# Row tiles for two small products, keys copied between halves by transfers, and an order table for the planner, in a two-layer attention trunk

## The chip, the core and the metric

The kernel runs on one core of a Trainium2 chip. The metric is the device time of one execution in microseconds; the time given for a kernel is the median of its runs. A core has a matrix engine (TensorE; PE in the profile, with its weight loads as PEld), a vector engine (VectorE, DVE), an activation engine (ScalarE, ACT), GpSimd (POOL) and a sync engine that issues most transfers (SyncE, SP). Each works through its own instructions in the order in which they were written.

## What is computed

Two residual layers over a sequence of 256 tokens of width 1024. Each takes shift, scale and gate from a condition vector, normalises, mixes, projects and adds. Cut to the places that the change touches:

```python
for i in range(DEPTH):                       # two layers
    shift, scale, gate = jnp.split(cond @ ada_w[i] + ada_b[i], 3, axis=-1)
    h = rms_norm(x, norm_g[i]) * (1 + scale[:, None, :]) + shift[:, None, :]
    y = nsa_mixer(h, ...) if i == 0 else moba_mixer(h, ...)
    x = x + gate[:, None, :] * y
# first layer: 16 query heads in 4 groups, three branches, each with its own keys
p_cmp = masked_softmax(q @ k_cmp * scale)    # 15 compressed blocks per group
o = g0 * (p_cmp @ v_cmp) + g1 * o_slc + g2 * o_win
y = (o * silu(z)) @ w_out
# second layer: one branch of plain causal attention, same grouping
y = (softmax(causal(q @ k * scale)) @ v * silu(z)) @ w_out
```

All inputs and the output are float32.

## The kernel before, in words

**Precision.** Large products are made of float32r parts: an operand is split into hi and lo, and a product is hi·hi + hi·lo + lo·hi, three one-pass matmuls (`product`, lines 757 to 766; `parts_of`, 624 to 631: ScalarE casts hi, VectorE subtracts lo). Small products are plain float32, which PE runs as two passes, so one instruction of the program appears as two in the trace.

**Stages.** The condition's modulation for layer one and the first projection run interleaved while weights stream in (to about 60 us). Then come the remaining projections of the first layer, with the compression network beside them; the first layer's attention over eight head pairs (`pair_a`, 1290 to 1331) with the z projection as filler; its output projection (`out_products`, 1370); the second layer's norm and projections; its attention (`pair_b`, 1439) with its z projection as filler; and the last output projection. The second layer's modulation (`ada_rows`, 640) runs beside the first layer's attention, column-tiled: four products of 32 output rows stand side by side in four column strips of the array (`tile_position=(0, 32 * j)`).

**Compressed values.** `compressed(hf)` (1262) makes, for four pairs at a time, the softmax over the compressed blocks and leaves it transposed in `pcT[hf]`, 128 rows: 32 rows for each of the four pairs, 16 for each head. The values are in `Vbd` (1239): for each half and pair a 128 x 128 matrix that is zero but for that pair's 32 rows, built with `emask`, eight columns of ones over 16 rows each. In `pair_a` line 1328 multiplies the whole 128 rows of `pcT` by the pair's matrix and opens the pair's output bank `o`, into which `values` (899) then adds the other two branches, column-tiled in two strips of 64. `gated` reads `o` and frees it.

**Gate spread.** `ada_gate(0)` (696) has the gate in four rows of a tile `g`, two partial sums and a bias row in each half. Lines 714 to 718 spread it to all 128 partitions with two matmuls against `selG`, whose two 128 x 128 matrices hold ones over the upper or the lower 64 rows.

**Second layer's keys.** `make_k` (820) normalises and rotates the keys, doubles each 64-wide key to 128 columns (`twice`), transposes four groups for each 128 tokens, so that both halves of the partitions hold the key, and splits the result into hi and lo in `KTB`, a view of the tile KTA. Both halves are needed because a query column holds its hi part over its lo part. The first layer's keys go the same way.

**What sets the order.** Nothing is issued while the program is written down: `Plan.record` collects operations, and `Plan.issue` (231) then simulates the engines with costs (`_cost`, 174) and picks, engine by engine, the ready operation that can start first, ties broken by level (`FIRST_OF_ALL`, `URGENT`, `CHAIN`, `FILL`) and then by the number under which the operation was recorded. It also hands out the tile buffers of each tag: `ps` has six PSUM banks and `acc` two, `raw` has five buffers for weights on their way in. A load waits until its buffer is free. All engine instructions thus carry one line in the profile, L373, the line of the planner that calls them.

Of the kernel before, what the change touches and what calls it, by code (L numbers as in the profile page):

```python
# [9 lines left out]
F32 = mybir.dt.float32  # L10
# [4 lines left out]
OP = mybir.AluOpType  # L15
# [21 lines left out]
DEEP = 2e4  # L37
TILED, LATER = -0.5, 0
SHORT_ROWS, SMALL, BEHIND, EARLY_RATE = 1.1, 7e4, 5500.0, 348.0
ISSUE, FIRST_BYTE, RATE, LANDED = 450.0, 1500.0, 315.0, 700.0  # L40

# [11 lines left out]
class Plan:  # L53
# [120 lines left out]
    def _cost(self, engine, method, args, kw, aps):  # L174
# [15 lines left out]
        if engine == "T":  # L190
            if method == "transpose":
                return 262.0 if aps[1].dtype == F32 else 180.0
            cols = free(aps[2])
            if aps[2].dtype == F32:
                m = free(aps[1])
                if "tile_position" in kw and m <= 64:
                    return max(cols * 4.28 * max(32, m) / P, 60.0)
                return 2 * max(cols * 2.14, 264.0)
            return max(cols * (1.07 if aps[2].dtype == F32R else 1.0), 264.0)
# [31 lines left out]
    def issue(self, opening=()):  # L231
# [46 lines left out]
        for op in ops:  # L278
            op["at"] = 0.0
            if not op["wait"]:  # L280
                ready[op["engine"]].append(op)
        done = 0
        while done < len(ops):
            best = None
            for e, ops_e in ready.items():
# [4 lines left out]
                for op in ops_e:  # L290
                    t = max(clock[e], op["at"])
                    if first is not None and t > first and not (op["level"] < 0 and t <= first + self.AHEAD):
                        continue
                    blocked = False
                    for n in op["needs"]:
                        r = room(n)
                        if r is None:
                            blocked = True
                            break
                        t = max(t, r)  # L300
                    if blocked:
                        continue
                    found.append((t, self._rank(op, e, mode), op["id"], op))
                    first = t if first is None else min(first, t)
# [28 lines left out]
            if e == "T":  # L333
                tick = int(start // TICK)
                if op["mode"] != mode:
                    cost += 240.0
                mode = op["mode"]
                cost = cost * (1 / 2.4 if tally.get(tick - 1, 0.0) >= 3060.0 else 1 / 1.2)
                tally[tick] = tally.get(tick, 0.0) + op["cost"]
            end = start + cost  # L340
            clock[e] = end
            seen = end + self.SEEN[e]
            if "bytes" in op:
                if e != "S":
                    seen = start + (BEHIND if op["level"] > 0 else 2400.0)
                else:
                    wire = max(wire, start + ISSUE + FIRST_BYTE) + op["bytes"] / (EARLY_RATE if start < 5e4 else RATE)
                    seen = wire + (450.0 if start < 5e4 else LANDED)
                    landings.append(seen)
                    if start < DEEP:  # L350
                        clock[e] = max(start + ISSUE, landings[-8] if len(landings) >= 8 else 0.0)
# [49 lines left out]
def kernel(  # L401
# [47 lines left out]
    plan.tag("early", early["pool"], 1024, 12)  # L449
    plan.tag("raw", work, 1024, 5)  # L450
    plan.tag("hi", work, 1024, 4, F32R)
# [76 lines left out]
    for m in range(2):  # L528
        keep(maskC[:, m, :], [[-16, 16]], m * P - 31)
    selG = const.tile([P, 2, P], F32, name="selG")  # L530
    nc.gpsimd.memset(selG, 0.0)
    nc.gpsimd.memset(selG[0:64, 0, :], 1.0)
    nc.gpsimd.memset(selG[64:128, 1, :], 1.0)
    ones = const.tile([P, P], F32, name="ones")
    nc.gpsimd.memset(ones, 1.0)
    identR = const.tile([P, P], F32R, name="identR")
    V.tensor_copy(identR, identF)
    emask = const.tile([P, 8], F32, name="emask")
    V.tensor_reduce(emask, identF.rearrange("p (j n) -> p j n", n=16), axis=AX.X, op=OP.add)

# [155 lines left out]
    def ada_gate(l):  # L696
# [12 lines left out]
        else:  # L709
            g = yield from ada_rows(l, (2 * D, 2 * D + 512), 512)  # L710
            for s in range(2):
                Q.dma_start(g[64 * s + 1:64 * s + 2], bias[:, s * 512:(s + 1) * 512])
            mix, src = (selG[:, 0], selG[:, 1]), (g, g)
        for s in range(2):
# [105 lines left out]
    def make_k(raw_k, kinds, kt_view, offs):  # L820
# [5 lines left out]
        norm_rope(src, 2 * n, KVH, TC[:, j0:j0 + n].rearrange("p c m d -> p (c m) d"),  # L826
                  TS[:, k0:k0 + n].rearrange("p c m d -> p (c m) d"), y)
        for j, off in enumerate(offs):
            twice = tile_of("y", KVH, 2 * HD)
# [408 lines left out]
    vb = tile_of("ps", 512)  # L1238
    Vbd = const.tile([P, 2, 4, P], F32, name="Vbd")
    for hf in range(2):  # L1240
        for cc in range(2):
# [4 lines left out]
                     start=(cc == 0), stop=(cc == 1))  # L1246
        V.tensor_mul(Vbd[:, hf].rearrange("p j (e d) -> p (j e) d", e=2),
                     vb[:, None, hf * HD:(hf + 1) * HD].to_broadcast([P, 8, HD]),
                     emask[:, :, None].to_broadcast([P, 8, HD]))

# [8 lines left out]

    pcT = {}  # L1260

# [28 lines left out]
    def pair_a(i):  # L1290
# [28 lines left out]
        for r in (1, 0):  # L1319
# [6 lines left out]
            pT.insert(0, p_transposed(block))  # L1326
        o = tile_of("ps", 512)
        T.matmul(o[:, 0:S], Vbd[:, hf, j_], pcT[hf], start=True, stop=False)
        vs = slice(g * HD, (g + 1) * HD)
# [171 lines left out]
```

## Time and profile before

| | us |
|---|---|
| median of 3 runs | 317.1 |
| lowest, highest run | 315.71, 317.89 |
| the profiled execution, its own time | 317.45 |
| its span, first to last instruction | 315.7 |

How to read it: a row of the timeline has its start, its length, the engine, the line, the operation, output tile <- input tiles, rows x columns of the stationary operand and of the output, and how many instructions it merges. Names are those of the tiles without their numbers: `ps` and `acc` are PSUM banks, `pT` transposed probabilities, `HT` the transposed layer input, `raw` weights as loaded, `hi` and `lo` their parts, `qg` queries, `condz` the condition. A shape `128*32` is a matmul in a column tile of 32, `128*64` one in a tile of 64. Ends of matmuls are modelled and overlap the next start. A row of busy times by stage has, for each engine, the busy time and the number of instructions.

### The profile page before, as it was taken

To read this page: it belongs to the slowest core of one execution; us is meant where nothing else is said; L and a number is where in the kernel's file an instruction comes from. 1 tells how busy PE (TensorE), PEld (TensorE's weight loads), DVE (VectorE), ACT (ScalarE), POOL (GpSimd) and SP (SyncE) were. 2 spreads that over 40 slices of the span, in tenths; PEclk is the share of its full clock that TensorE was granted. 3 is DMA by queue.
4 is the path that set the end of the run, shared out by engine and by line. 5 is a ranking of instruction groups with operands and counts; after the bars stand their busy time and mean duration, and the time that the engine had idled before them with its cause. 6 is when DMAs were issued, how large, how long until landed. Compare 5 with 4: busy or idle time off the path is not lost.

```text
span 315.7 us, 6158 instructions
## 1 busy us (share of the span) xinstructions
PE 306.0 (97%) x2133; PEld 243.5 (77%) x2133; DVE 242.2 (77%) x734; ACT 205.0 (65%) x486; POOL 26.6 (8%) x102
## 2 busy tenths in 40 slices
PE   4999999998999999999999999999999999999995
PEld 4666677777766797858879888877788999968784
DVE  4673374669982899835979887998599999999764
ACT  5735155764835787456799966786486489998420
POOL 8248900000000000000000000000000000000000
PEclk9999999999999999999999999999999999999999
DMA  7999999359899822788272377617188862423102
GB/s 248 320 357 367 368 359 323 111 171 311 279 309 306 277 79 90 246 304 250 113 261 76 116 217 226 240 60 212 65 261 263 298 229 84 155 69 120 59 34 102
DMA packets 44174, 65.82 MB, mean 208 GB/s; under 512 B 4221, under 2 KB 20971, under 8 KB 44142
## 3 DMA queue, kind: packets, MB, share of 16 engines
q1 hardware_dynamic: 43782, 65.36, 63.1%
q8 instruction: 17, 0.28, 0.4%
q14 instruction: 15, 0.12, 0.1%
q10 hardware_dynamic: 168, 0.06, 0.1%
q0 software_dynamic: 192, 0.00, 0.0%
HBM read 64.36 MB, written 1.05 MB: 207 GB/s over the span
## 4 chain that ended last, share of the span: by engine, by line
PE 90%; DMA 5%; ACT 2%; DVE 1%; issue 1%; SPq 0%; ACTq 0%; DVEq 0%
PE ps L373 54%; PE acc L373 36%; DMA raw<-in_nsa_w_in_dram 2%; DMA early<-in_ada_w_dram 2%; ACT hi L373 1%; DMA rot<-in_c_dram 0%; ACT n_in L373 0%; DVE lo L373 0%; DVE p L373 0%; ACT p L373 0%; DVE AB L373 0%; ACT HT L373 0%; DVE rot L373 0%; DVE y L373 0%; DVE X L373 0%
## 5 line engine op out<-in xcount | busy, mean ns | idle before, releaser
L373 ACT CAST hi<-raw 128x1024 fp32r<-128x1024 f32 (+1 forms) x48 | 48.8, 1023 | 25.5 <-DMA raw<-in_nsa_w_in_dram 9.8
L373 DVE TENSOR_TENSOR lo<-raw,hi 128x1024 fp32r<-128x1024 f32 (+1 forms) x48 | 56.4, 1181 | 11.0 <-ACT hi L373 10.8
L373 PE MATMUL acc<-hi,HT 128*128 128x512 f32 (+1 forms) x160 | 49.6, 381 | 1.3 <-ACT n_in L373 0.8
L373 ACT ACTIVATE p<-p,tiny 128x128 f32<-128x128 f32 (+1 forms) x96 | 43.2, 460 | 8.4 <-DVE tiny L373 8.3
L373 PE MATMUL acc<-HT,hi 128*128 128x256 f32 x192 | 37.8, 286 | 0.0
L373 PEld LDWEIGHTS acc<-hi,HT 128*128 128x128 f32 x160 | 29.1, 188 | 9.6 <-issue 2.9
L373 DVE CUSTOM_DVE_ANT_0 p<-ps,causal 128x128 f32<-128x128 f32 (+1 forms) x96 | 30.5, 346 | 3.1 <-PE ps L373 3.1
L373 PEld LDWEIGHTS acc<-HT,hi 128*128 128x128 f32 x192 | 30.1, 188 | 0.8 <-issue 0.7
L373 PE MATMUL acc<-lo,HT 128*128 128x512 f32 (+1 forms) x80 | 30.2, 380 | 0.2 <-DVE lo L373 0.2
L373 PE MATMUL ps<-hi,HT 128*128 128x512 f32 (+1 forms) x96 | 28.2, 365 | 0.0
L373 PE MATMUL acc<-HT,lo 128*128 128x256 f32 x96 | 27.8, 290 | 0.0
L373 PE MATMUL ps<-KTA,qg 128*128 128x256 f32 (+2 forms) x192 | 27.0, 284 | 0.0
L373 ACT COPY pT<-ps 128x384 f32<-128x384 f32 x48 | 21.5, 485 | 6.3 <-PE ps L373 6.2
L373 PEld LDWEIGHTS ps<-KTA,qg 128*128 128x128 f32 x192 | 24.2, 190 | 1.7 <-issue 1.2
L373 PE MATMUL ps<-hi,qg 128*128 128x256 f32 (+1 forms) x96 | 24.1, 323 | 0.0
L373 PE MATMUL acc<-hi,qg 128*128 128x512 f32 x64 | 22.8, 402 | 0.0
L373 PE MATMUL ps<-identF,p 128*128 128x128 f32 x144 | 21.7, 276 | 0.0
L373 PEld LDWEIGHTS ps<-hi,HT 128*128 128x128 f32 x96 | 17.0, 188 | 4.2 <-issue 2.1
L373 PEld LDWEIGHTS ps<-identF,p 128*128 128x128 f32 x144 | 16.4, 140 | 3.9 <-issue 1.2
L373 ACT ACTIVATION_READ_ACCUMULATOR p<-p,tiny 128x1 f32 x96 | 19.3, 201 | 0.0
L373 PE MATMUL ps<-pT,VA 128*64 128x256 f32 (+1 forms) x192 | 19.1, 334 | 0.0
L373 PEld LDWEIGHTS acc<-HT,lo 128*128 128x128 f32 x96 | 18.1, 189 | 0.1
(223 smaller groups left out, 614.5 us busy)
## 6 DMA issues: line engine op xcount, KB each, us to landing
raw<-in_ada_w_dram SPq DMA_DIRECT2D x32, 512.0 KB, 4.9
raw<-in_moba_w_in_dram SPq DMA_DIRECT2D x20, 512.0 KB, 4.3
early<-in_ada_w_dram SPq DMA_DIRECT2D x12, 512.0 KB, 9.5
raw<-in_nsa_w_in_dram SPq DMA_DIRECT2D x12, 512.0 KB, 6.4
early<-in_nsa_w_in_dram SPq DMA_DIRECT2D x9, 512.0 KB, 9.1
p<-in_nsa_cmp_w_dram SPq DMA_DIRECT2D x16, 256.0 KB, 3.8
raw<-in_nsa_w_out_dram SPq DMA_DIRECT2D x8, 512.0 KB, 5.7
raw<-in_moba_w_out_dram SPq DMA_DIRECT2D x8, 512.0 KB, 4.8
```

The lines of the kernel that those rows point to most:

```text
L373: r = getattr(self.engines[e], method)(*[self._real(a) for a in args], **{k: self._real(a) for k, a in kw.items()})
```

## The change

Four edits to the program and a set of edits to the planner.

1. `Vbd` loses its pair index: one 128 x 128 matrix for each half, in which every pair's 32 rows hold that pair's values side by side. `emask` becomes two columns. In `pair_a` of the first of four pairs, four products are issued as one group: each takes 32 rows of `Vbd` and of `pcT` in its own row tile (`tile_position=(32 * j, 0)`) and opens its own bank, `ov[hf, j]`. The four banks of a half are therefore open at once.
2. `ada_gate(0)` spreads the gate with two matmuls in row tiles of 64 rows against plain ones; `selG` goes.
3. In `make_k`, for the second layer, two groups' keys (128 columns) are transposed at once, so four transposes are left of eight. The upper 64 partitions of a result hold the even groups, the lower the odd ones. Each half is split into hi and lo in place, and a transfer on GpSimd's queue copies it to the other 64 partitions, 128 KB at a time, four transfers.
4. `raw` gets a sixth buffer.
5. The planner: a table `LATER_BY` shifts the rank of some 160 operations by so many places, a table `HOLD` keeps 16 from being picked before a set time, costs are changed (row tiles, a pause at each tick, the new transfers), and an operation that needs several banks waits for all of them.

```diff
-TILED, LATER = -0.5, 0
+TILED, LATER, PAUSE = -0.5, 0, 93.0
...
+LATER_BY = [
+    (123, 129, 27), (139, 145, 112), (248, 249, -64), (308, 310, -90), (384, 387, -43), (404, 404, -43),
...
+HOLD = {
+    309: 22600, 390: 48700, 434: 55900, 651: 89000, 689: 116600, 1059: 131000, 1335: 168400, 1559: 195200,
...
-            op["at"] = 0.0
+            op["at"], op["key"] = HOLD.get(op["id"], 0.0), op["id"] + SHIFT.get(op["id"], 0)
...
+                    for name, several in new.items():
+                        if len(several) > 1 and not blocked:
+                            free = sorted(self.tags[name].free)
+                            blocked = len(free) < len(several)
+                            t = t if blocked else max(t, free[len(several) - 1][0])
...
-                    found.append((t, self._rank(op, e, mode), op["id"], op))
+                    found.append((t, self._rank(op, e, mode), op["key"], op))
...
-    plan.tag("raw", work, 1024, 5)
+    plan.tag("raw", work, 1024, 6)
...
-    selG = const.tile([P, 2, P], F32, name="selG")
...
-    emask = const.tile([P, 8], F32, name="emask")
-    V.tensor_reduce(emask, identF.rearrange("p (j n) -> p j n", n=16), axis=AX.X, op=OP.add)
+    emask = const.tile([P, 2], F32, name="emask")
+    V.tensor_reduce(emask, identF.rearrange("p (j e n) -> p e j n", e=2, n=16), axis=AX.XY, op=OP.add)
...
-            mix, src = (selG[:, 0], selG[:, 1]), (g, g)
+            ts = [tile_of("ps", 512) for s in range(2)]
+            with plan.at(FILL):
+                with plan.group():
+                    for s in range(2):
+                        T.matmul(ts[s], ones[64 * s:64 * s + 64], g[64 * s:64 * s + 64], start=True, stop=True,
+                                 tile_position=(64 * s, 0))
+                for s in range(2):
+                    A.copy(gate[:, s * 512:(s + 1) * 512], ts[s])
+            return
...
+        if n == 1:
+            KT32 = kt_view.bitcast(F32)
+            for j, off in enumerate(offs):
+                t = tile_of("ps", 2, P)
+                with plan.group():
+                    for gp in range(2):
+                        T.transpose(t[:, gp], y[:, 4 * j + 2 * gp:4 * j + 2 * gp + 2].rearrange("p g d -> p (g d)"), identF)
+                for e in range(2):
+                    own, other = slice(64 * e, 64 * e + 64), slice(64 - 64 * e, 128 - 64 * e)
+                    hi, lo = (kt_view[own, part, e::2, off:off + P] for part in range(2))
+                    A.copy(hi, t[own])
+                    V.tensor_sub(lo, t[own], hi.bitcast(F32))
+                    G.dma_start(KT32[other, :, e::2, off:off + P], KT32[own, :, e::2, off:off + P])
+            return
...
-    Vbd = const.tile([P, 2, 4, P], F32, name="Vbd")
+    Vbd = const.tile([P, 2, P], F32, name="Vbd")
...
-        o = tile_of("ps", 512)
-        T.matmul(o[:, 0:S], Vbd[:, hf, j_], pcT[hf], start=True, stop=False)
+        if j_ % 4 == 0:
+            with plan.group():
+                for j in range(j_, j_ + 4):
+                    ov[hf, j] = tile_of("ps", 512)
+                    T.matmul(ov[hf, j][:, 0:S], Vbd[32 * j:32 * j + 32, hf], pcT[hf][32 * j:32 * j + 32],
+                             start=True, stop=False, tile_position=(32 * j, 0))
+        o = ov[hf, j_]
```

How the order of instructions moves, at three places. First the compressed values on PE, in the first layer's attention, before (the numbers are buffers):

```order
L373 MATMUL ps_156<-pcT_1542,Vbd 128x256
L373 MATMUL ps_162<-identF,p_714 128x128
L373 MATMUL ps_162<-identF,p_712 128x128 x2
L373 MATMUL ps_212<-identF,row_249 128x128 x4
L373 MATMUL ps_156<-pT_1389,VA 64x256
L373 MATMUL ps_156<-pT_1257,VA 64x256
```

and now:

```order
L408 MATMUL acc_272<-HT,hi_329 128x256
L408 MATMUL ps_208<-pcT_1554,Vbd 128x256
L408 MATMUL ps_238<-pcT_1554,Vbd 128x256
L408 MATMUL ps_158<-pcT_1554,Vbd 128x256
L408 MATMUL ps_152<-pcT_1554,Vbd 128x256
L408 MATMUL ps_208<-pT_1364,VA 64x256
L408 MATMUL ps_208<-pT_1373,VA 64x256
```

A product that stood alone ahead of each pair's values now stands with three others ahead of the first pair's, in four banks; the same comes once more for the other half.

Second, the values of the second layer's attention on PE, before:

```order
L373 MATMUL acc_283<-HT,hi_334 128x256
L373 MATMUL ps_196<-identR,n_parts_1050 128x128 x4
L373 MATMUL ps_156<-pT_1300,VA 64x256
L373 MATMUL ps_156<-pT_1257,VA 64x256
L373 MATMUL ps_156<-pT_1300,VA 64x128
L373 MATMUL ps_156<-pT_1257,VA 64x128
L373 MATMUL ps_212<-KTA,qg_1094 128x256 x4
L373 MATMUL acc_283<-HT,lo_346 128x256
```

and now:

```order
L408 MATMUL ps_220<-KTA,qg_1467 128x256 x4
L408 MATMUL ps_192<-pT_1386,VA 64x256
L408 MATMUL ps_192<-pT_1364,VA 64x256
L408 MATMUL ps_192<-pT_1386,VA 64x128
L408 MATMUL ps_192<-pT_1364,VA 64x128
L408 MATMUL ps_152<-pT_1373,VA 64x256
L408 MATMUL ps_152<-pT_1379,VA 64x256
L408 MATMUL ps_152<-pT_1373,VA 64x128
L408 MATMUL ps_152<-pT_1379,VA 64x128
L408 MATMUL ps_158<-KTA,qg_1467 128x128 x4
```

Two pairs' column-tiled values follow each other directly, here and in three more places; before, each pair's stood alone, in eight places. Over the whole program PE goes from whole-array matmuls into tiled ones 38 times before and 35 times now, and from one tile shape directly into another 10 times before and 7 now.

Third, the second layer's key transposes on PE, before:

```order
L373 MATMUL acc_276<-hi_309,HT 128x512
L373 MATMUL ps_224<-identF,y_143 128x128 x4
L373 MATMUL ps_242<-identF,y_217 128x128 x4
L373 MATMUL acc_276<-hi_309,HT 128x512
L373 MATMUL acc_276<-lo_315,HT 128x512
```

and now, followed by the end of GpSimd's own list, where the copies are its last instructions:

```order
L408 MATMUL acc_279<-hi_329,HT 128x512
L408 MATMUL ps_152<-identF,n_out_281 128x128 x2
L408 MATMUL ps_220<-identF,n_out_281 128x128 x2
L408 MATMUL acc_279<-lo_311,HT 128x512
L408 MATMUL acc_279<-hi_329,HT 128x512 x2
L408 DMA KTA<-KTA 64x4x128 x4
```

Eight transposes are four, `twice` is gone, and between the last of them and the first row of PE that reads the second layer's keys stand 130 matmuls.

More of the change, by code (lines that the diff above doesn't have):

```diff
@@ L37 @@
 DEEP = 2e4
-TILED, LATER = -0.5, 0
+TILED, LATER, PAUSE = -0.5, 0, 93.0
 SHORT_ROWS, SMALL, BEHIND, EARLY_RATE = 1.1, 7e4, 5500.0, 348.0
-ISSUE, FIRST_BYTE, RATE, LANDED = 450.0, 1500.0, 315.0, 700.0
+ISSUE, FIRST_BYTE, RATE, LANDED, MOVED = 450.0, 1500.0, 315.0, 700.0, 2500.0
+LATER_BY = [
[13 rows of a table added]
+]
+SHIFT = {i: d for a, b, d in LATER_BY for i in range(a, b + 1)}
+HOLD = {
+    309: 22600, 390: 48700, 434: 55900, 651: 89000, 689: 116600, 1059: 131000, 1335: 168400, 1559: 195200,
+    1574: 198900, 1581: 200600, 1588: 203800, 1636: 205300, 1648: 209400, 1653: 209900, 1887: 230100, 2333: 284700,
+}
 class Tag:
@@ L194, in _cost @@
             if aps[2].dtype == F32:
-                m = free(aps[1])
-                if "tile_position" in kw and m <= 64:
-                    return max(cols * 4.28 * max(32, m) / P, 60.0)
+                m, rows = free(aps[1]), aps[1].shape[0]
+                if "tile_position" in kw and m * rows <= 64 * P:
+                    return max(cols * 4.28 * max(32, m) / P * max(32, rows) / P, 60.0) + (100.0 if rows < P else 0.0)
                 return 2 * max(cols * 2.14, 264.0)
@@ L300, in issue @@
                         t = max(t, r)
+                    new = {}
+                    for n in op["needs"]:
+                        if self.tiles[n]["slot"] is None:
+                            new.setdefault(self.tiles[n]["tag"].name, []).append(n)
+                    for name, several in new.items():
[3 more added lines that the diff above has]
+                            t = t if blocked else max(t, free[len(several) - 1][0])
                     if blocked:
                         continue
-                    found.append((t, self._rank(op, e, mode), op["id"], op))
+                    found.append((t, self._rank(op, e, mode), op["key"], op))
                     first = t if first is None else min(first, t)
@@ L339, in issue @@
                 tally[tick] = tally.get(tick, 0.0) + op["cost"]
+                if (start + cost) // TICK > tick:
+                    cost += PAUSE
             end = start + cost
@@ L345, in issue @@
                     seen = start + (BEHIND if op["level"] > 0 else 2400.0)
+                    if start > 5e4:
+                        wire = max(wire, start + ISSUE + FIRST_BYTE) + op["bytes"] / RATE
+                        seen = wire + MOVED
                 else:
@@ L529 @@
         keep(maskC[:, m, :], [[-16, 16]], m * P - 31)
-    selG = const.tile([P, 2, P], F32, name="selG")
-    nc.gpsimd.memset(selG, 0.0)
-    nc.gpsimd.memset(selG[0:64, 0, :], 1.0)
-    nc.gpsimd.memset(selG[64:128, 1, :], 1.0)
     ones = const.tile([P, P], F32, name="ones")
@@ L1246 @@
                      start=(cc == 0), stop=(cc == 1))
-        V.tensor_mul(Vbd[:, hf].rearrange("p j (e d) -> p (j e) d", e=2),
-                     vb[:, None, hf * HD:(hf + 1) * HD].to_broadcast([P, 8, HD]),
-                     emask[:, :, None].to_broadcast([P, 8, HD]))
+        V.tensor_mul(Vbd[:, hf].rearrange("p (e d) -> p e d", e=2),
+                     vb[:, None, hf * HD:(hf + 1) * HD].to_broadcast([P, 2, HD]),
+                     emask[:, :, None].to_broadcast([P, 2, HD]))
     raw_q = tile_of("n_in", 2, 512)
@@ L1257 @@
     z_later = z_blocks(w_in, 3120, zT)
-    pcT = {}
+    pcT, ov = {}, {}
     def compressed(hf):
```

12 rows, old and new, of the table LATER_BY are left out of this document.

## The prediction

> **What bounds the kernel now.** I read the page first, then who waits for whom, then the busy time by stage, then TensorE's timeline.
>
> ```profile
> span 315.7 us, 6158 instructions
> ...
> PE 306.0 (97%) x2133; PEld 243.5 (77%) x2133; DVE 242.2 (77%) x734; ACT 205.0 (65%) x486; POOL 26.6 (8%) x102
> ...
> PEclk9999999999999999999999999999999999999999
> ...
> PE 90%; DMA 5%; ACT 2%; DVE 1%; issue 1%; SPq 0%; ACTq 0%; DVEq 0%
> ```
>
> TensorE (PE) is busy for 97% of the span, at the full granted clock in every slice, and 90% of the chain that ended last runs on it. A busy PE here is one that is handed the next matmul before the last has drained, so below I read a cost from one start to the next, not from the length of an instruction. Now the waits of PE, in all, times, longest:
>
> ```profile
> PE ps L373 <- POOL selP L512: 2.3, 1, 2.3
> PE ps L373 <- DMA X<-in_x_dram: 1.7, 1, 1.7
> PE acc L373 <- ACT n_in L373: 0.8, 1, 0.8
> PE acc L373 <- ACT HT L373: 0.5, 1, 0.5
> PE ps L373 <- DVE p L373: 0.3, 1, 0.3
> PE acc L373 <- DVE lo L373: 0.2, 1, 0.2
> PE ps L373 <- ACT n_in L373: 0.2, 1, 0.2
> ```
>
> The first two (4.0 us) are the start and the change doesn't touch them. The other five sum to 2.0 us in the whole rest. So the time is the sum of what PE issues; it falls when PE's work falls, as long as what feeds PE keeps up. Whether it can, stage by stage (columns: PE, weight load, VectorE, ScalarE, GpSimd busy, clock, DMA share, GB/s):
>
> ```profile
> 98.00:183.00 85.00, 85.00 (x716) 68.83 (x716) 67.84 (x294) 65.45 (x203) 0.00 (x0) 1.00 0.56 187
> 183.00:245.00 62.00, 61.74 (x310) 50.43 (x309) 51.82 (x103) 43.31 (x77) 0.00 (x0) 1.00 0.61 193
> 245.00:285.00 40.00, 40.00 (x336) 36.46 (x336) 39.66 (x140) 33.09 (x91) 0.00 (x0) 1.00 0.51 170
> ```
>
> In the first layer's attention (98 to 183) VectorE has 17 us to spare and ScalarE 20. In the second layer's (245 to 285) VectorE is busy for 39.66 of 40: there a second engine stands as close to the limit as PE, and I come back to it.
>
> **The change, part by part.** Compressed values. A product of pcT and Vbd is two passes of 256 columns over the whole array:
>
> ```profile
> 102.96 1.11 PE L373 MATMUL ps<-KTA,qg 128*128 128x256 f32 x8
> 104.00 1.08 PE L373 MATMUL ps<-p,p 128*64 128x256 f32 x8
> ...
> 142.62 0.60 PE L373 MATMUL ps<-pcT,Vbd 128*128 128x256 f32 x2
> 142.86 0.82 PE L373 MATMUL ps<-KTA,qg 128*128 128x256 f32 x4
> 143.61 1.52 PE L373 MATMUL ps<-pT,VA 128*64 128x256 f32 x16
> 145.06 1.06 PE L373 MATMUL ps<-raw,condz 128*32 128x512 f32 x8
> 146.06 1.21 PE L373 MATMUL ps<-KTA,qg 128*128 128x256 f32 x8
> ```
>
> One product, four KTA products and the turn into column tiles take 143.61 - 142.62 = 0.99. Eight KTA products and such a turn take 104.00 - 102.96 = 1.04, so four with it lie between 0.52 and 0.57, and a compressed product costs 0.42 to 0.47; I take 0.43. Eight of them are 3.44 us. After the change four stand in four row tiles, twice. No row-tiled run of any size is in this trace; the nearest row is the column-tiled one:
>
> ```profile
> 130.01 1.92 PE L373 MATMUL ps<-raw,condz 128*32 128x512 f32 x16
> 131.87 0.55 PE L373 MATMUL ps<-identF,p 128*128 128x128 f32 x3
> ```
>
> Sixteen column-tiled passes take 1.86, eight take 1.00 (145.06 to 146.06): eight more cost 0.86, or 0.11 for a pass of 512 columns, where a whole-array pass of that size takes 0.43 (the gate rows below). Four run at once. If row tiles do the same, the eight products cost 2 x 0.43 = 0.86, saving 2.6 us; if they run one behind the other, nothing. I take 2.6, since the nearest row shows full overlap and the new order gives the four different banks.
>
> The Trainium skill ("TensorE: Matmul & The Clock Gate", "Part 3: Packing small matmuls — row/col tiling") reports a speedup of 3.07 for four row tiles of 32 rows, not 4. As an estimate from that page the eight would cost 3.44 / 3.07 = 1.12 and the end come 0.26 us later; no run here shows it yet.
>
> Gate spread. Two products of 512 columns, four passes:
>
> ```profile
> 119.48 1.88 PE L373 MATMUL ps<-row,selG 128*128 128x512 f32 x4
> 121.19 0.49 PE L373 MATMUL ps<-identF,p 128*128 128x128 f32 x3
> ```
>
> They take 1.71. In two row tiles of 64 rows side by side: 0.86, saving 0.85 (0 if they don't overlap). The memsets of selG leave POOL, which is idle in every stage shown above.
>
> Second layer's keys. Eight transposes become four:
>
> ```profile
> 235.48 1.03 PE L373 MATMUL ps<-identF,y 128*128 128x128 f32 x8
> 236.27 0.47 PE L373 MATMUL acc<-hi,HT 128*128 128x512 f32 x1
> ...
> 236.12 1.07 ACT L373 CAST KTA<-ps 128x512 fp32r<-128x512 f32 x2 [0.41 <-PE ps L373]
> ...
> 257.37 2.99 PE L373 MATMUL ps<-KTA,qg 128*128 128x128 f32 x24
> 260.20 0.28 PE L373 MATMUL acc<-HT,hi 128*128 128x256 f32 x1
> ```
>
> Eight took 0.79, so 0.4 is saved. New is the copy between halves: four transfers on POOL's queue, each behind the cast and the subtraction of its half. Nothing else stands behind them on that queue, and POOL does no other work then. Here the keys were cast by 237.2 and first read at 257.37. In the new order 130 matmuls, about 18 us at the rates of the trace, still lie between the key transposes and the first scores. POOL's transfers of the start landed after this long:
>
> ```profile
> rs<-in_positions_dram POOLq DMA_DIRECT2D x1, 1.0 KB, 4.1
> y<-in_nsa_gate_b_dram POOLq DMA_DIRECT2D x1, 0.2 KB, 5.1
> ```
>
> Four to 5 us, even twice that for 128 KB, is covered by the 18. Cost 0; without that cover it would be 5 us of PE, as the first scores stand in PE's own order. ScalarE loses two doubling copies and its casts are cut in quarters; VectorE's work there stays.
>
> Turns between tile shapes. The order table moves tiled runs together. In the second layer's attention eight separate visits to column tiles become four of double length. One visit, with its edges:
>
> ```profile
> 272.33 1.08 PE L373 MATMUL ps<-KTA,qg 128*128 128x128 f32 x8
> 273.34 0.87 PE L373 MATMUL ps<-pT,VA 128*64 128x256 f32 x8
> 274.14 0.38 PE L373 MATMUL acc<-HT,hi 128*128 128x256 f32 x1
> 274.36 0.29 PE L373 MATMUL acc<-HT,lo 128*128 128x256 f32 x1
> 274.48 0.40 PE L373 MATMUL acc<-HT,hi 128*128 128x256 f32 x2
> ```
>
> Going in: the eight KTA before it took 1.01, and at the 2.83 / 24 of the row at 257.37 they would take 0.94, so 0.07. Inside: 0.80 for eight passes here, 1.45 for sixteen (143.61 to 145.06), so 0.15 is not streaming. Coming out: 0.22 to the next start where 0.12 is usual, 0.10. A visit costs 0.32, and four fewer save 1.3. But they lie in the stage where VectorE is full: I take half, 0.65 (0 to 1.3). In the rest of the program visits go from 30 to 31 and direct changes from one tile shape to another from 10 to 7, the new row-tiled runs among them: +0.32 - 0.45, taken as 0.
>
> Waits. Of the 2.0 us of PE's waits a new order can remove all or bring others; a sixth raw buffer lets loads run further ahead. I take 0.5 saved (2.0 saved to 1.5 lost).
>
> Sum: 2.6 + 0.85 + 0.4 + 0.65 + 0.5 = 5.0. The profiled execution took 317.45 (1.7 around its span), so 312.45; from the median of the runs shown, 317.1, it is 312.1. I forecast **312.2 us**.
>
> **The rivals.** VectorE binds in the second layer. For it: 39.66 of 40. Against it: the new order starts the first scores before the first half of the z products is done, where before they came after it, which spreads that work. If it binds, the 0.65 and the 0.5 are gone: 317.45 - 3.85 = 313.6.
>
> Row tiles don't overlap. For it: the trace shows only column tiles doing so. Then 2.6 and 0.85 fall away: 317.45 - 1.55 = 315.9.
>
> New waits. The order of 155 loads and of hundreds of instructions changes, and each engine works in order. Double today's 2.0 us of waits, and the gain is 4.5 - 2.0 = 2.5: 315.0; triple, 317.0. I price it at 316. Against it: VectorE's and ScalarE's slack up to 245.
>
> PSUM banks held, the case on the other side. The change opens four output banks at once and closes them one pair after the other; ps has six banks, and the modulation of the second layer holds one more. Until the pairs end, transposes and scores share what is left. In the new order I count 14 places in these two stretches where a bank is written again after only 0.88 to 1.35 us of PE's work, 1.16 on average. What such a bank needs to come free is in these rows:
>
> ```profile
> L373 ACT COPY pT<-ps 128x384 f32<-128x384 f32 x32 | 14.4, 482 | 3.9 <-PE ps L373 3.8
> ...
> 160.11 0.49 PE L373 MATMUL ps<-identF,p 128*128 128x128 f32 x3
> ...
> 160.75 0.48 ACT L373 COPY pT<-ps 128x384 f32<-128x384 f32 x1
> ```
>
> Transposes that end at 160.60 are copied out by 161.23, 0.63 later; 1.16 covers that. Were the round trip 1.5 us (two 0.48 copies queued ahead), 14 x 0.36 = 5.0 would eat the gain; from about 1.7 the kernel is over 1% slower; at 1.85 the loss is 9.7 and the time 317.45 - 5.0 + 9.7 = 322. The Trainium skill ("TensorEngine Tiling (Array Packing)", "Gotcha 1: PSUM Pressure") warns of this: row tiles must write different banks. No run here shows the price.
>
> **How the numbers follow.** Forecast 0.62; VectorE binds 0.14; new waits 0.11; banks held 0.07; no overlap 0.06. One per cent, about what a measurement of this kernel can tell from no change, is 3.2 us: faster means under 313.9. The forecast lies there nearly always, VectorE's case a little over half the time: 0.60 + 0.08 = 0.68. Slower than 320.3 is nearly only the banks' case, with a little of the new waits: 0.08. The rest, 0.24, is within 1%. Low end of the range: every term at its best, 2.6 + 0.85 + 0.4 + 1.3 + 2.0 = 7.15, 310.3, less about 1 for waits hidden inside busy time: 309.0. High end: 316.5, taking in no overlap and most of new waits; beyond lie the banks' case and the worst of the waits.
>
> **What would show it.** Right: eight Vbd passes that start four at a time and end together, a run of them near 0.45 us plus a turn; the gate's four passes in about 0.9; half as many column-tiled visits after 245; PE's waits after the start at 2 us or less; the transfers of KTA landing well ahead of the first scores. Wrong: Vbd passes 0.2 us apart; PE waiting for ScalarE's pT copies or VectorE's maxima between 115 and 160; PE waiting for VectorE after 245 with VectorE full; new waits for raw loads. A time over 314 means that one of the rivals holds.

## The result, and the profile after

The changed kernel takes **313.6 us** (median of 4 runs, 313.09 to 314.04) beside 317.36 for the kernel before; the ratio is 0.9902, with a 95% interval of 0.988 to 0.9925. The forecast was 312.2 with a range of 309.0 to 316.5: the direction and the range hold, but of the 5 us that the sum gave, 3.1 to 3.8 came. A second measurement, beside the experiments, gave 313.58 against 316.70, ratio 0.9896 (0.9878 to 0.9914): 3.1 us, and I use that one below. The profiled execution of before, on which the sum was made, stands 0.75 above that median of 316.70; a part of the missing gain is this and needs no cause.

The busy times of the changed kernel, and the waits of PE in it:

```profile
PE 302.0 (97%) x2129; PEld 241.8 (78%) x2129; DVE 242.4 (78%) x736; ACT 205.0 (66%) x486; POOL 30.0 (10%) x103
```

```profile
PE ps L408 <- POOL selP L547: 2.3, 1, 2.3
PE ps L408 <- DMA X<-in_x_dram: 1.6, 1, 1.6
PE ps L408 <- ACT p L408: 0.6, 1, 0.6
PE acc L408 <- ACT HT L408: 0.5, 1, 0.5
PE ps L408 <- ACT pT L408: 0.4, 1, 0.4
PE ps L408 <- DVE lo L408: 0.2, 1, 0.2
PE ps L408 <- DMA p<-in_nsa_cmp_w_dram: 0.2, 1, 0.2
```

PE is as full as before, 302.0 us instead of 306.0 with VectorE's and ScalarE's work unchanged. Without the two waits of the start the waits sum to 1.9, where they were 2.0: other places, the same total. The second layer's attention (columns as in the prediction):

```profile
241.00:283.00 42.00, 41.96 (x354) 38.48 (x354) 41.97 (x144) 35.35 (x99) 0.00 (x0) 1.00 0.50 165
```

VectorE is now busy there for 41.97 of 42 us. Where the time was won shows in PE's timeline. The first pair of rows here is the gate, the next three the first run of compressed values, the last three the second layer's key transposes:

```profile
111.04 1.13 PE L408 MATMUL ps<-row,ones 64*128 64x512 f32 x4
112.10 0.44 PE L408 MATMUL ps<-identF,g 128*128 128x128 f32 x2
...
136.68 0.40 PE L408 MATMUL acc<-HT,hi 128*128 128x256 f32 x2
137.00 0.71 PE L408 MATMUL ps<-pcT,Vbd 32*128 32x256 f32 x8
137.65 1.52 PE L408 MATMUL ps<-pT,VA 128*64 128x256 f32 x16
...
229.42 0.63 PE L408 MATMUL acc<-hi,HT 128*128 128x512 f32 x2
230.08 0.66 PE L408 MATMUL ps<-identF,n_out 128*128 128x128 f32 x4
230.49 0.48 PE L408 MATMUL acc<-lo,HT 128*128 128x512 f32 x1
```

The gate takes 1.06 where it took 1.71. Eight compressed passes take 0.65 from the first start to the next work's, and the pair ahead of them 0.32 where two such passes usually take 0.23: 0.09 for going in. Two such runs cost 2 x (0.65 + 0.09) = 1.5, where eight products of 0.43 cost 3.44. The four transposes take 0.41, but PE starts them 0.66 after a pair that usually takes 0.46.

And where nothing was won: the second layer, from the first row of its z products on HT,lo to the last row of PE. Before, then after:

```profile
242.66 0.28 PE L373 MATMUL ps<-HT,lo 128*128 128x256 f32 x1
...
311.89 0.28 PE L373 MATMUL ps<-hi,qg 128*128 128x256 f32 x1
```

```profile
238.72 0.28 PE L408 MATMUL ps<-HT,lo 128*128 128x256 f32 x1
...
307.99 0.28 PE L408 MATMUL ps<-hi,qg 128*128 128x256 f32 x1
```

69.23 us before, 69.27 after. All of the gain stands ahead of this stage; the turns that were to be saved in it gave nothing. That is what the experiments had to explain. Ahead of it the two traces differ by 3.94 us (242.66 and 238.72), more than the rows above add up to. But executions with the same work up to here differ by as much as 1 us: the light version of the kernel before, shown below, reaches this row at 241.66 and is 0.99 ahead already after 106 us, long before the work that it leaves out.

### The profile page after: what moved, and what is told of

Its sections match the earlier page's. It is cut to its first block, busy times and chain, and to the rows that moved or that the text cites. A ratio compares the mean times of both kernels' runs of the same rounds, so it can differ in the third digit from the quotient of the medians.

```text
span 311.8 us, 6168 instructions
## 1 busy us (share of the span) xinstructions
PE 302.0 (97%) x2129; PEld 241.8 (78%) x2129; DVE 242.4 (78%) x736; ACT 205.0 (66%) x486; POOL 30.0 (10%) x103
## 4 chain that ended last, share of the span: by engine, by line
PE 89%; DMA 6%; DVE 3%; issue 1%; ACT 1%; SPq 0%; DVEq 0%; ACTq 0%
PE ps L408 52%; PE acc L408 36%; DMA raw<-in_nsa_w_in_dram 2%; DMA p<-in_nsa_cmp_w_dram 2%; DVE lo L408 1%; DMA X<-in_x_dram 1%; DVE p L408 1%; SPq L408 0%; ACT p L408 0%; DVE AB L408 0%; ACT hi L408 0%; ACT pT L408 0%; ACT HT L408 0%; DVE rot L408 0%; DVE y L408 0%
## 5 line engine op out<-in xcount | busy, mean ns | idle before, releaser
L408 PE MATMUL ps<-KTA,qg 128*128 128x256 f32 (+2 forms) x192 | 27.8, 283 | 0.0
L408 PE MATMUL ps<-hi,qg 128*128 128x256 f32 (+1 forms) x96 | 23.3, 322 | 0.0
L408 ACT CAST hi<-early 128x1024 fp32r<-128x1024 f32 (+2 forms) x17 | 15.0, 897 | 11.2 <-DMA early<-in_nsa_w_in_dram 8.6
L408 PE MATMUL acc<-hi,qg 128*128 128x512 f32 x64 | 21.9, 401 | 0.0
L408 DVE TENSOR_TENSOR lo<-early,hi 128x1024 fp32r<-128x1024 f32 (+2 forms) x17 | 17.3, 1034 | 5.4 <-ACT hi L408 5.4
L408 ACT COPY pT<-ps 128x384 f32<-128x384 f32 x48 | 20.5, 485 | 1.4 <-PE ps L408 1.2
L408 POOL DMA_DIRECT2D KTA<-KTA x4 | 2.5, 642 | 191.3 <-DVE KTA L408 191.3
L408 PE MATMUL ps<-identF,p 128*128 128x128 f32 x144 | 20.2, 276 | 0.4 <-ACT pT L408 0.4
```

Source lines behind the costliest of these rows:

```text
L408: r = getattr(self.engines[e], method)(*[self._real(a) for a in args], **{k: self._real(a) for k, a in kw.items()})
```

## The experiments

Four runs ask where the gain comes from, three more repeat this from the other side, and five ask why the second layer gave nothing and what a row tile costs. In those that keep the changed kernel's order, this order was written into the kernel as a list of operations, or the costs in the planner were left as they were.

**Row tiles undone, products still together.**

```diff
-                    T.matmul(ov[hf, j][:, 0:S], Vbd[32 * j:32 * j + 32, hf], pcT[hf][32 * j:32 * j + 32],
-                             start=True, stop=False, tile_position=(32 * j, 0))
+                    T.matmul(ov[hf, j][:, 0:S], Vbd[:, hf], pcT[hf], start=True, stop=False)
```

> The changed kernel with its order untouched; only the four row-tiled compressed products of each half are made as four products over the whole array at the same place (all 128 rows of Vbd and pcT, without the mask of the other pairs, so that the compressed part of the first layer's output mixes four pairs). Theory A (what the row tiles save is matmul time: four at once): each half's run of eight passes goes from 0.65 us to 8 x 0.216 = 1.73, about +1.0 us a half with the turn into tiles, +2.0 in all: 315.6 us. Rival B (the gain is the order, the products being gathered or the table): at most +0.5: 314.1 or less.

Measured: 315.48 us (9 runs, 313.97 to 316.15), ratio to before 0.9949 (0.9928 to 0.997); 1.9 above the changed kernel. Its trace:

```profile
137.49 1.91 PE L408 MATMUL ps<-pcT,Vbd 128*128 128x256 f32 x8
139.33 1.52 PE L408 MATMUL ps<-pT,VA 128*64 128x256 f32 x16
...
166.82 1.99 PE L408 MATMUL ps<-pcT,Vbd 128*128 128x256 f32 x8
168.75 1.52 PE L408 MATMUL ps<-pT,VA 128*64 128x256 f32 x16
```

1.84 and 1.93 us instead of 0.65 and 0.64: 2.5 more, or 2.3 without the 0.09 that each tiled run costs ahead of it, where the medians say 1.9; their intervals leave room for both. Theory A holds, B falls: it is the side-by-side passes that save, not the gathering.

**The products back at their pairs.** The same matmuls, but three of each four issued ahead of their own pair's values, in a bank opened there.

```diff
+        o = tile_of("ps", 512)
         if j_ % 4 == 0:
-            with plan.group():
...
-        o = ov[hf, j_]
+            T.matmul(o[:, 0:S], Vbd[:, hf], pcT[hf], start=True, stop=False)
+        else:
+            with plan.added():
+                T.matmul(o[:, 0:S], Vbd[:, hf], pcT[hf], start=True, stop=False)
```

> The changed kernel with every other instruction in the changed kernel's order, but each pair's compressed product over the whole array and back ahead of its own pair's values, as before the change (without the mask, as in the run before). Theory A: a product costs 0.43 wherever it stands, so the same +2.0 to +2.4 us, 315.6 to 316.0. Rival B (gathering matters): 1 us or more above the gathered version. Rival C (banks held cost something): below the gathered version, since banks are opened one at a time.

Measured: 315.94 us (12 runs), ratio 0.9966 (0.9947 to 0.9985), 0.5 above the gathered version, with intervals that overlap. Theory A. B's 1 us isn't there, and neither is C: opening the banks one at a time made nothing faster, so holding four costs nothing that shows here (the intervals leave room for a few tenths).

**The gate over the whole array.**

```diff
-                        T.matmul(ts[s], ones[64 * s:64 * s + 64], g[64 * s:64 * s + 64], start=True, stop=True,
-                                 tile_position=(64 * s, 0))
+                        T.matmul(ts[s], ones, g, start=True, stop=True)
```

> The changed kernel with its order untouched; only the gate spread is two products over the whole array instead of two row tiles (against plain ones, so that both halves of the gate get the sum of both). Theory A: its four passes go from 1.06 us to 1.72, +0.65: 314.2 us. Rival B: no change, 313.6.

Measured: 314.79 us (6 runs, 313.48 to 315.07), ratio 0.9927 (0.9903 to 0.9951): 1.2 above. The direction is A's, the size isn't settled. In its trace the four passes start at 110.70 and the next work at 112.52, but PE's wait of 0.4 for pT is gone and that execution, 313.56, is no longer than the changed kernel's. A longer gate can be hidden by such a wait; in four of the six runs something more was lost that the one trace doesn't show.

**No tables in the planner.**

```diff
-LATER_BY = [
...
+LATER_BY = []
...
-HOLD = {
...
+HOLD = {}
```

> The changed kernel with both tables of the planner empty (no shifted ranks, no holds); all other edits stay, and the planner orders by level and number as before. Theory A (the gain is matmul work removed, and the turns saved in the second layer were given back): within 1 us of 313.6, some waits of PE more. Rival B (the table carries the gain): 315.5 or more, with the visits to column tiles after the second layer's scores back at seven or eight.

Measured: 315.4 us (12 runs, 314.63 to 316.45), ratio 0.9959 (0.9942 to 0.9975). That is 1.8 above the changed kernel, nearly what B asked; A expected at most 1. Where:

```profile
238.55 0.28 PE L391 MATMUL ps<-HT,lo 128*128 128x256 f32 x1
...
251.24 1.57 PE L391 MATMUL ps<-identR,n_parts 128*128 128x128 f32 x16 [0.94 <-DVE n_parts L391]
...
309.29 0.28 PE L391 MATMUL ps<-hi,qg 128*128 128x256 f32 x1
```

It reaches the z products as early as the changed kernel (238.55 and 238.72) and then takes 70.74 us, 1.5 more than either of the two others. So the table isn't seen to have shortened what stands ahead of them. It repairs what the other edits (the new costs and pauses among them; which one wasn't tried) do to the second layer's order: the query parts come 0.94 us late from VectorE, and the eight separate visits are back.

**The changed kernel once more.**

> The changed kernel as it is, once more, as the measure for the runs beside it. All theories: 313.6 us within 0.5, and the same places as in its first profile: the z products of the second layer start at 238.6 in the trace and TensorE ends 69.7 us later.

Measured: 313.58 us (5 runs), as said above. From the first z product on HT,lo (238.12) to the end of PE 69.55 us, as in the first trace (69.54).

**The second layer's keys as before.**

```diff
-        if n == 1:
-            KT32 = kt_view.bitcast(F32)
...
-            return
```

> The changed kernel in its own order, but the second layer's keys made as before the change: doubled by two ScalarE copies, eight transposes, casts over all partitions, no transfers. Theory A (matmul work counts): four more transposes at 0.11 us, +0.4: 314.0 us. Rival B (the shorter group stands alone and pays its edges, 0.20 ahead and 0.09 behind in the changed kernel's trace, against 0.08 behind before): +0.2 or less, 313.8. Rival C (the copies between halves are late or disturb the loads): faster than the changed kernel.

Measured: 314.0 us (6 runs, 312.86 to 315.07), ratio 0.9913 (0.9891 to 0.9935). 0.4 above, with ranges that overlap: not told from nothing. Its trace is worth more:

```profile
231.13 1.18 PE L514 MATMUL ps<-identF,y 128*128 128x128 f32 x8 [0.67 <-ACT y L514]
...
240.29 0.28 PE L514 MATMUL ps<-HT,lo 128*128 128x256 f32 x1
...
308.79 0.28 PE L514 MATMUL ps<-hi,qg 128*128 128x256 f32 x1
```

PE lost 0.67 waiting for ScalarE's doubling copy, and the stretch around the transposes took 1.16 more in all (2.23 from 229.84 to 232.07, where the changed kernel takes 1.07 from 229.42 to 230.49). From the z products on it took 68.50 instead of 69.27: 0.77 of the 1.16 came back, 0.54 of it by the first product of the query parts (`n_parts`), which comes 8.85 after the first z product instead of 9.39. In six executions of the changed order with VectorE's work untouched (the changed kernel twice, products gathered, products apart, gate whole, four rounds) the stage takes 69.23 to 69.28, with the query parts at 9.38 to 9.40; so 0.77, though of one trace, is clear of that scatter. A stage that gives back what was lost ahead of it is held by something other than PE.

**The row tiles alone, in the kernel before.** Only `Vbd`, `emask`, the grouped products and the rule for several banks.

```diff
+            with plan.group() as four:
+                for j in range(j_, j_ + 4):
+                    ov[hf, j] = tile_of("ps", 512)
+                    T.matmul(ov[hf, j][:, 0:S], Vbd[32 * j:32 * j + 32, hf], pcT[hf][32 * j:32 * j + 32],
+                             start=True, stop=False, tile_position=(32 * j, 0))
```

> The kernel before with one edit of the change alone: compressed values of four pairs in four row tiles, four banks opened at once (and the planner's rule that such an operation waits for all its banks). No table, five raw buffers, old gate and keys. Theory A (four at once save about 2 us of matmul): 2.0 below the kernel before, 314.7 us against 316.75. Rival B (held banks make transposes and scores wait without a table that places them): 316 or more, with waits of PE on pT copies between 135 and 170.

Measured: 314.8 us (12 runs, 313.91 to 316.59), ratio 0.9937 (0.9915 to 0.9959): 1.9 below the kernel before, and no wait of PE for pT in its list. Theory A, from both sides now: 1.9 taken away from one kernel, 1.9 given to the other. The planner orders this kernel anew, so the order around the products differs too; the run at 132.98 takes 0.65 to the next start at 133.63, as in the changed kernel.

**Less work for VectorE, in the changed kernel and in the one before.** The same edit in both, each in its own order:

```diff
-                    V.scalar_tensor_tensor(gate, w, condz[:, kk, 0:1], gate, op0=OP.mult, op1=OP.add)
+                    V.scalar_tensor_tensor(gate[:, 0:32], w[:, 0:32], condz[:, kk, 0:1], gate[:, 0:32], op0=OP.mult, op1=OP.add)
```

> The changed kernel in its own order, with the eight VectorE multiply-adds of the second layer's gate cut from 1024 to 32 columns, which takes about 9 us of work from VectorE between 241 and 300 and leaves the gate of the other columns out. Theory A (PE bounds the second layer, its visible waits there are 0.2 us): 0.2 to 0.4 lower, 313.3. Rival V (VectorE, busy for 41.97 of 42 us, holds the second layer and ate what the saved turns gave): 0.7 or more lower, 312.9 or less.

> The kernel before in its own order, with the same eight VectorE multiply-adds cut from 1024 to 32 columns (the gate of the other columns is left out). The changed kernel gained 0.9 us by this. Theory V (only in the changed order does VectorE hold TensorE, and so it ate what the saved turns gave): 0.3 or less below the kernel before, 316.4 or more. Rival U (a full VectorE costs the second layer about the same in either order, so it explains no part of the missing gain): 0.7 to 1.2 below, 315.5 to 316.0.

Measured: changed kernel 312.65 us (6 runs), ratio to before 0.9872 (0.9853 to 0.9891), 0.9 lower than with the work. Kernel before 316.48 (6 runs) against 316.69, ratio 0.9993 (0.9952 to 1.0035): no difference, though this interval alone can't exclude 1 us. The traces are sharper. The 46 us from the first z product on HT,lo (changed; changed and light; before; before and light):

```profile
238.72:284.72 46.00, 45.96 (x388) 42.12 (x387) 45.73 (x158) 39.00 (x104) 0.00 (x0) 1.00 0.53 170
```

```profile
237.71:283.71 46.00, 46.00 (x392) 42.73 (x390) 41.73 (x156) 39.62 (x107) 0.00 (x0) 1.00 0.53 178
```

```profile
242.66:288.66 46.00, 46.00 (x384) 41.79 (x383) 45.56 (x160) 39.01 (x106) 0.00 (x0) 1.00 0.50 166
```

```profile
241.66:287.66 46.00, 46.00 (x385) 41.78 (x383) 39.70 (x157) 39.39 (x108) 0.00 (x0) 1.00 0.49 163
```

VectorE is full in both kernels and PE too, so busy time doesn't tell them apart. From the same first row to PE's last start it does: light and changed 237.71 to 306.00, light and before 241.66 to 310.70:

```profile
306.00 0.28 PE L514 MATMUL ps<-hi,qg 128*128 128x256 f32 x1
```

```profile
310.70 0.28 PE L479 MATMUL ps<-hi,qg 128*128 128x256 f32 x1
```

68.29 and 69.04 us. Relieving VectorE takes 0.98 off the changed kernel's second layer and 0.19 off the old one's. The 0.98 is clear of the scatter of the changed order (69.23 to 69.28); the 0.19 isn't told from nothing, since the kernel before with row tiles alone, whose visits in this stage are the same, takes 69.53. Counted from the first z product, the light changed kernel is 0.20 ahead at the first query parts (9.19 and 9.39), 0.43 at the second (19.95 and 20.38) and 0.98 at the output projection's first 512-column product on the weights' lo part into a `ps` bank (46.03 and 47.01): it gains where PE uses what VectorE makes.

With VectorE out of the way the changed order is 0.75 shorter than the old one. The saved turns are in this, but not alone. Inside the visits PE's own rows show them, in the changed kernel with its full load too: eight of 0.80 (6.40) became three of 1.45 and one of 1.49 (5.84), so 0.56 less, with the ends besides; and the stage is no shorter. In the old light kernel weight loads also wait for ScalarE's p (0.9) and pT (0.7), which they don't in the changed light one. Theory V holds. The waits of PE itself don't show it, because here it is the weight loads that wait; in the view of who waits for whom, for PEld from 237 to 300, the changed kernel has

```profile
PEld ps L408 <- DVE lo L408: 0.6, 2, 0.4
```

and the light one has no such row. This row is not the whole of the 0.98: the kernel with doubled keys has the same 0.6 in it and a stage of 68.50.

**The gate's multiply-adds on GpSimd.**

```diff
-                    V.scalar_tensor_tensor(gate, w, condz[:, kk, 0:1], gate, op0=OP.mult, op1=OP.add)
+                    with plan.group():
+                        G.tensor_scalar_mul(w, w, condz[:, kk, 0:1])
+                        G.tensor_add(gate, gate, w)
```

> The changed kernel with every other instruction in its order; the eight multiply-adds of the second layer's gate run on GpSimd instead of VectorE, as a product in place and an addition, nothing left out. Theory V or U (VectorE's load costs the second layer 0.9 us): 312.7 us. Rival B (GpSimd is too slow: it holds the raw buffers longer, or the gate's product at 277 waits for it, and the work it does disturbs VectorE): 314 or more, with PE waiting for POOL or for raw loads after 235.

Measured: 333.0 us (6 runs, 331.39 to 335.29), ratio 1.0507 (1.0458 to 1.0557). B, and far worse than B said. Its groups on POOL (230 to 290); on VectorE the query parts and the 256-column scalings (busy, mean ns), first in the changed kernel from 241 to 283, then here from 245 to 285; PE's longest waits; and two stages:

```profile
L514 POOL TENSOR_SCALAR raw<-raw,condz 128x1024 f32<-128x1024 f32 x7 | 21.4, 3062 | 14.8 <-DMA raw<-in_ada_w_dram 12.3 <-DVE rot L514 2.4
L514 POOL TENSOR_TENSOR gate<-gate,raw 128x1024 f32<-128x1024 f32 x7 | 17.5, 2493 | 0.6
```

```profile
L408 DVE TENSOR_TENSOR n_parts<-n_out,n_parts 128x512 fp32r<-128x512 f32 x4 | 2.6, 685 | 0.0
L408 DVE TENSOR_SCALAR p<-p,tiny 128x256 f32<-128x256 f32 x12 | 3.7, 347 | 0.0
```

```profile
L514 DVE TENSOR_TENSOR n_parts<-n_out,n_parts 128x512 fp32r<-128x512 f32 x4 | 6.6, 1684 | 0.4 <-ACT n_parts L514 0.4
L514 DVE TENSOR_SCALAR p<-p,tiny 128x256 f32<-128x256 f32 x4 | 4.9, 1239 | 0.0
```

```profile
PE ps L514 <- DVE n_parts L514: 7.1, 2, 5.0
PE ps L514 <- DVE p L514: 4.5, 3, 2.4
```

```profile
245.00:265.00 20.00, 15.01 (x106) 14.80 (x105) 17.01 (x41) 11.43 (x26) 13.92 (x6) 0.74 0.63 217
265.00:285.00 20.00, 13.42 (x100) 11.66 (x100) 19.12 (x48) 10.77 (x32) 13.64 (x5) 0.83 0.01 1
```

A piece takes 3.06 + 2.49 us on GpSimd where VectorE took 1.27, and VectorE's own instructions beside it lengthen: the query parts from 685 to 1684 ns, the 256-column scaling from 347 to 1239. PE waits for both, and the granted clock, 1.00 here in the changed kernel, falls to 0.74 and 0.83. The Trainium skill ("SBUF — State Buffer", "SBUF: two separate sides") says that GpSimd and VectorE share one pair of ports to the memory as an exclusive lock, which a VectorE instruction takes when it reads two operands from SBUF or runs in a two-port mode, and that the loser waits for a whole instruction of the other. The trace agrees: the product of `n_in` and `rs`, which reads two operands, also grew, from 1223 to 2005 ns, while the masking of scores `p<-ps,causal`, which takes one operand from a PSUM bank, kept its 413 ns (412 here). That the scaling, with one such operand, runs in a two-port mode is not shown.

**One scaling of four on ScalarE.**

```diff
+                if m and e:
+                    A.activation(pm[m][:, e], pm[m][:, e], AF.Copy, scale=sm[:, m, e:e + 1])
+                else:
+                    V.tensor_scalar_mul(pm[m][:, e], pm[m][:, e], sm[:, m, e:e + 1])
```

> The changed kernel with every other instruction in its order; in the second layer, one of each pair's four scalings of the probabilities (the 256-column one of the second head, about 0.37 us on VectorE) runs on ScalarE, eight in all. Nothing is left out. Theory V (VectorE's load holds the second layer in the changed order; 9 us off gave 0.9): 3 us off give 0.3 or a little more, 313.2 us or less. Rival B (ScalarE's scalings of about 0.4 us stand ahead of the pT copies, which TensorE's values wait for): 314 or more, with PE waiting for ACT pT after 250.

Measured: 314.61 us (6 runs, 313.31 to 315.24), ratio 0.9929 (0.9911 to 0.9947): 1.0 above. B's time, though by another wait: not the copies of pT, but the transposes, whose input now comes from ScalarE. The changed kernel, then this one:

```profile
261.52 0.82 PE L408 MATMUL ps<-identF,p 128*128 128x128 f32 x6
262.10 1.16 PE L408 MATMUL ps<-KTA,qg 128*128 128x128 f32 x8
```

```profile
262.00 1.18 PE L514 MATMUL ps<-identF,p 128*128 128x128 f32 x6
262.94 1.17 PE L514 MATMUL ps<-KTA,qg 128*128 128x128 f32 x8
```

Six transposes take 0.94 where the changed kernel has 0.58 (261.52 to 262.10). VectorE was relieved, and the work landed on a chain that PE stands right behind. No version here with all its work is clearly faster than the changed kernel.

**Four rounds instead of two.**

```diff
+                for c in range(2):
+                    for j in range(j_, j_ + 4):
+                        T.matmul(ov[hf, j][:, c * P:(c + 1) * P], Vbd[32 * j:32 * j + 32, hf],
+                                 pcT[hf][32 * j:32 * j + 32, c * P:(c + 1) * P],
+                                 start=(c == 0), stop=False, tile_position=(32 * j, 0))
```

> The changed kernel in its own order, with each row-tiled compressed product cut into two of 128 columns, so that a half takes four rounds of four passes instead of two. Theory A (each round in row tiles pays about 0.1 us on top of its columns: 0.32 for 256 columns where a pass over the whole array takes 0.216): a run of sixteen takes 4 x 0.21 = 0.83 us instead of 0.65, +0.4 us in all, 314.0. Rival B (the 0.2 us are paid once, going in and coming out): a run stays at 0.65 and the time at 313.6.

Measured: 313.52 us (6 runs, 313.15 to 313.76), ratio 0.9887 (0.9853 to 0.9921): no change.

```profile
136.61 0.73 PE L408 MATMUL ps<-pcT,Vbd 32*128 32x128 f32 x16
137.27 0.44 PE L408 MATMUL ps<-pT,VA 128*64 128x256 f32 x2
```

Sixteen passes of 128 columns take 0.66, eight of 256 took 0.65. Theory A falls: a round costs its columns and nothing more. About 0.22 of a run of 0.65 (0.65 - 2 x 0.216) is paid once, at its two ends.

## Why the prediction was right in direction and too large in size

**PE bounds the kernel.** Right up to the second layer: the whole-array products put back are 2.3 us more of PE by the rows and cost 1.9 by the medians, and taken out of the kernel before they gain 1.9.

**Compressed values, -2.6.** The streaming was right: four at once, no loss between rounds. What the run pays at its ends (0.22 inside, 0.09 ahead) I had counted among "the rest of the turns", where it was set off to 0; it wasn't. By the rows 3.44 - 1.5 = 1.9, and 1.9 by the medians of both experiments. The estimate worked out from the Trainium skill ("TensorE: Matmul & The Clock Gate", "Part 3: Packing small matmuls — row/col tiling"), 1.12 us at a speedup of 3.07, was nearer than mine: run against run it is 3.77 / 1.29 = 2.9 here.

**Gate, -0.85.** 0.65 in the trace, for the same reason. The time of the kernel without it says 1.2; the size stays open.

**Key transposes, -0.4, and the copies, 0.** Four instead of eight saved 0.38, of which the late start of the four, 0.20, takes half: 0.2. The copies were hidden, as predicted, with more to spare than needed: four of 128 KB, 4.3 us from issue to landing, the last issue at 234.9, the first scores at 249.51:

```profile
KTA<-KTA POOLq DMA_DIRECT2D x4, 128.0 KB, 4.3
```

```profile
249.51 1.60 PE L408 MATMUL ps<-KTA,qg 128*128 128x128 f32 x12
```

**Turns in the second layer, -0.65 of 1.3.** This is the step that failed. The visits went from eight to four as the order said, and PE's rows have 0.56 less inside them; the changed order is worth 0.75 by the light kernels, close to the half that I took. But I had taken the half as a discount for VectorE being full, and VectorE took the whole: 69.27 us against 69.23. The rival "VectorE binds in the second layer" named 313.6 for this, with a chance of 0.14. Its mechanism was right; that its time came out to a tenth is luck. It kept 3.85 for the other terms, which the rows put at 2.75, and it started from 317.45, 0.75 above the later median; the two errors largely cancel. The sign in the profile was already there: 39.66 of 40. My own signs would have missed it: a time over 314 can't show a rival priced at 313.6, and I looked for PE waiting, where it is the weight loads that wait. Against it I had held that the scores start earlier. They do (10.8 us after the first z product instead of 14.7: 249.51 and 257.37 in the rows of KTA), but VectorE stays busy for 45.73 of the 46 us after it, so nothing of its load went away by that.

**Waits, -0.5.** Gone in name, not in sum: 2.0 and 1.9. The wait for n_in went and one for p came. The table, which I credited with these two terms, is worth 1.8 by the medians, 1.5 of it in the second layer, but against an order that the other edits had made worse.

**The rivals.** Row tiles that don't overlap: excluded. New waits: 1.9 in all, no. Banks held: no price seen; PE waited once, 0.4, for pT in the first trace and not in the second, and the kernel that opens its banks singly wasn't faster. (By the 1.16 of that paragraph a round trip of 1.5 costs 14 x 0.34 = 4.8, not 14 x 0.36; nothing hangs on it.)

The sum as the rows give it: 1.9 + 0.65 + 0.2 + 0 + 0.1 = 2.9, beside the 3.1 between the medians of 316.70 and 313.58. The pair of traces from which the rows come has 3.9; the 1 us between is about what two executions with the same work differ by, and no row accounts for it.

## What to carry to other kernels

Where two engines are both full in a stage, work taken off one of them can be worth nothing until the other is relieved, as here, and a discount of a half is a guess; test it by cutting the other engine's work in both kernels and comparing the stage, from one named instruction to another, in the traces. Cost a tiled run as its columns plus its two ends, about 0.3 us here, and count the ends where the run is new. Before moving work to an idle engine, ask what it shares with the full one, and who stands directly behind the moved instruction.

## What the runs showed of the hardware that was not expected

The same pass of 256 columns runs at two steady rates. In the changed kernel's z products and in those of before:

```profile
239.07 0.28 PE L408 MATMUL ps<-HT,lo 128*128 128x256 f32 x1
...
247.20 0.28 PE L408 MATMUL ps<-HT,lo 128*128 128x256 f32 x1
```

```profile
243.01 0.28 PE L373 MATMUL ps<-HT,lo 128*128 128x256 f32 x1
...
251.17 0.28 PE L373 MATMUL ps<-HT,lo 128*128 128x256 f32 x1
```

69 passes in 8.13 us, 118 ns each, and 72 in 8.16, 113 ns, both at a granted clock of 1.00 and both without a wait. It isn't tied to the order: the run with whole-array products gathered has the changed kernel's order and the fast rate there, and its second layer is as long, since PE then waited 0.4 for the query parts, which come 9.38 after its first z product, as they come 9.39 after it in the changed kernel. What sets the rate stays open.
